# A decoder layer on one core: modulation order, 20 up-projection halves ahead, V moved ahead of sparse attention

## The chip, the cores and the metric

The kernel runs on one core of a Trainium2 chip. The time is device microseconds of one execution, from the first to the last instruction with what lies around them; a lower time is better. The core has a matrix engine (PE, with its weight loads as PEld), a vector engine (DVE), a scalar engine (ACT), a queue (SP) that issues all loads here, and 16 DMA engines.

## The reference

One decoder layer on 256 positions of width 2048, with a condition vector c that scales, shifts and gates each part (six times 2048 columns of modulation). Attention has eight stick-breaking heads and eight heads of sparse attention with an indexer; the feed-forward part has 43 pairs (gate and value) of 128 columns, a causal convolution of width 3, and a down-projection.

```python
mod = jax.nn.silu(c) @ w_ada[l] + b_ada[l]
sh1, sc1, g1, sh2, sc2, g2 = jnp.split(mod[:, None, :], 6, axis=-1)
h = rmsnorm(x, norm1_g[l]) * (1.0 + sc1) + sh1
proj = h @ w_in[l]
...
o_sb = stick_breaking_attention(q_sb, k_sb, v_sb).reshape(B, S, SB_WIDTH)
...
o_ds = dsa_attention(q_ds, k_ds, v_ds, q_ix, k_ix, w_ix * idx_scale).reshape(B, S, DSA_WIDTH)
merged = jnp.concatenate([rmsnorm(o_sb, sb_norm_g[l]), rmsnorm(o_ds, dsa_norm_g[l])], axis=-1)
x = x + g1 * (merged @ w_out[l])
h2 = rmsnorm(x, norm2_g[l]) * (1.0 + sc2) + sh2
x = x + g2 * conv_ffn(h2, w_up[l], conv_w[l], conv_b[l], w_down[l])
```

## The kernel before

Everything is held transposed, 128 features on the partitions and 256 positions along the free side. All weights are float32 and come once from HBM, in loads of 1 MB (`load`, L135) into a ring of four buffers `raw`. Each load is split (`split`, L143) into a high part, a cast on ACT (L149), and a low part, a difference on DVE (L150), for three products per tile. `nat` (L153) and `trn` (L175) issue them as three matmuls, `trn` with 256 columns each; `fold` (L161) puts two of them into one matmul with 512 columns (L172), with the low weights at 256 columns (L170), and needs two PSUM banks per pair.

The modulation has 96 tiles of 128 columns, numbered 0 to 95: sh1, sc1, g1, sh2, sc2, g2, 16 each. Most are single columns of `ada` (L227): one load `wa` and one DVE instruction with an accumulator (L229). Five groups of four columns (`PEG`, starting at 4, 40, 48, 76 and 52) are done on PE by `ada_pe` (L198): four loads `wg`, four matmuls on four column strips after each (L206), a copy on ACT (L211), four transposes (L214) and a sum on DVE. Where these pieces fall is written out by hand: `pump` (L382) is called after each load or step and takes as many single columns and group quarters as the next digit of the two strings of `PLAN` says, and by fixed rates afterwards. `need` (L395) emits a column that is due at once.

The stages follow each other: the first projection over the first eight feature tiles (A, then A2, V and QK, pass 0) and over the other eight (A and A2, pass 1; `do_A` L412, `do_V` L461, `do_QK` L467); sparse attention (rotary, index scores, top-k, softmax) with PSUM pool `psB`, four banks `acc` for projections and four `att` for attention; V and QK of pass 1 with one stick-breaking head (`sb_head`, L670) after each QK; the output projection in eight tiles O, whose first half needs only the sparse heads (`do_O`, L714; four tiles are started ahead); the residual (`resid`, L738) and its norm (`rms_b`, L109); `h2_make` (L772), which makes one of 16 tiles of h2 from two columns of modulation; the up-projection U (`do_U`, L804); and the down-projection W. For the first `G0` = 8 pairs, `do_U(f, 0)` over features 0 to 7 runs ahead, while h2 of features 8 to 15 is still being made; each of these pairs keeps one of eight PSUM banks until `do_U(f, 1)`.

Tile's scheduler sets the order of each engine's instructions when the kernel is built: of those it takes to be ready it issues the one that comes first in the program.

## Time and profile before

| | us |
|---|---|
| median of 3 runs (1203.34 to 1205.74) | 1203.6 |
| the profiled execution | 1204.37 |
| its span, first to last instruction | 1202.6 |
| PE busy | 1150.5 |
| DVE busy | 880.1 |
| ACT busy | 635.3 |
| mean granted clock of PE | 0.982 |

Busy time is the time in which an engine has at least one instruction under way. A granted clock of 1.00 is 2.4 GHz, of 0.50 is 1.2 GHz. In a timeline row the number in brackets at the end is the idle time of that engine just before, and what ended it.

### The profile page before, as it was taken

Reading aid. Unit: us, or ns where it says so; the run is one execution under the profiler, and the core shown is the slowest. Engines: PE = TensorE matmul, PEld = TensorE weight load, DVE = VectorE, ACT = ScalarE, POOL = GpSimd, SP = SyncE. Lnnn points to the kernel's source line nnn. Section 1 sums busy time; section 2 is a strip of 40 time slices with the busy share of each in tenths; the row PEclk is TensorE's granted clock in tenths of the full one; section 3 lists DMA queues with packets and bytes.
Section 4 is the critical chain, followed back from the end, with each engine's and each line's share of the span. In section 5 each row is a group of like instructions: output and inputs, shape, how many; then the busy total and the mean of one; then the engine's idle time right before and its main releaser. Section 6 shows DMA issues by size and latency. Waiting matters only on the chain.

```text
span 1202.6 us, 17743 instructions
## 1 busy us (share of the span) xinstructions
PE 1150.5 (96%) x7120; PEld 1014.9 (84%) x7120; DVE 880.1 (73%) x1267; ACT 635.3 (53%) x1004; POOL 0.2 (0%) x4
## 2 busy tenths in 40 slices
PE   4699999899999998999999999999999999999996
PEld 2578997668879997999888888888888888888885
DVE  4886788699868888978788878787787645545453
ACT  3356554458566444556665565565556544444441
POOL 0000000000000000000000000000000000000000
PEclk9799999999999998999999999999999999999998
DMA  8988989758788796966578657565665555455531
GB/s 321 365 322 318 340 331 350 288 198 328 279 314 321 295 344 250 353 227 231 187 283 313 229 207 264 211 241 213 242 214 184 201 180 202 179 193 193 181 135 70
DMA packets 43283, 303.49 MB, mean 252 GB/s; under 512 B 4928, under 2 KB 5440, under 8 KB 7232
## 3 DMA queue, kind: packets, MB, share of 16 engines
q1 hardware_dynamic: 43200, 302.35, 68.2%
q8 instruction: 56, 0.92, 0.3%
q14 instruction: 27, 0.22, 0.0%
HBM read 300.24 MB, written 2.10 MB: 251 GB/s over the span
## 4 chain that ended last, share of the span: by engine, by line
PE 91%; DVE 4%; ACT 3%; DMA 1%; issue 1%; SPq 0%; DVEq 0%
PE U L172 21%; PE W L172 13%; PE U L170 11%; PE W L170 7%; PE U L178 3%; PE U L179 3%; PE QK L177 3%; PE U L177 3%; PE O L177 3%; PE O L179 3%; PE O L178 3%; PE QK L178 3%; PE QK L179 3%; PE A L155 2%; DVE wa L229 2%; PE A L156 2%
## 5 line engine op out<-in xcount | busy, mean ns | idle before, releaser
L229 DVE SCALAR_TENSOR_TENSOR wa<-wa,scb 128x2048 f32<-128x2048 f32 x76 | 173.4, 2284 | 2.2 <-DMA wa<-wa 2.1
L848 ACT COPY u<-U 128x256 f32<-128x256 f32 x70 | 26.1, 372 | 116.6 <-PE U L172 116.6
L849 DVE TENSOR_TENSOR u<-U,u 128x256 f32<-128x256 f32 x70 | 29.4, 420 | 58.7 <-ACT u L848 58.7
L859 DVE SCALAR_TENSOR_TENSOR uc<-u,par,uc 128x255 f32<-128x255 f32 (+1 forms) x140 | 63.8, 478 | 0.9
L855 ACT ACTIVATE uc<-u,par 128x256 f32<-128x256 f32 x70 | 41.9, 601 | 0.0
L866 ACT CAST aT<-uc 128x256 fp32r<-128x256 f32 x43 | 17.4, 404 | 33.3 <-DVE uc L865 33.3
L894 DVE SCALAR_TENSOR_TENSOR x1T<-W,mod,x1T 128x256 f32<-128x256 f32 x16 | 7.7, 482 | 31.1 <-PE W L170 31.1
L745 ACT ACTIVATE x2q<-x1T 128x256 f32<-128x256 f32 x15 | 6.3, 418 | 38.7 <-DVE x1T L740 38.6
L327 ACT ACTIVATE amul<-mod,b,par 128x1 f32<-128x1 f32 x32 | 12.0, 385 | 27.7 <-DVE wa L229 27.7
L206 PE MATMUL ap<-wg,csil 128*32 128x512 f32 x160 | 24.0, 657 | 0.7 <-DMA wg<-wg 0.4
L861 ACT ACTIVATE uc<-uc 128x256 f32<-128x256 f32 x43 | 17.9, 416 | 7.7 <-DVE uc L859 7.6
L330 ACT ACTIVATE mod<-mod,par 128x1 f32<-128x1 f32 x32 | 8.7, 295 | 24.0 <-DVE wa L229 22.9
L865 DVE TENSOR_TENSOR uc<-uc 128x256 f32<-128x256 f32 x43 | 18.2, 423 | 2.8
L867 DVE TENSOR_TENSOR aT<-uc,aT 128x256 fp32r<-128x256 f32 x43 | 18.0, 418 | 0.8 <-ACT aT L866 0.7
L859 DVE SCALAR_TENSOR_TENSOR uc<-U,par,uc 128x255 f32<-128x255 f32 (+1 forms) x32 | 15.0, 478 | 1.0 <-ACT uc L855 0.6
L206 PEld LDWEIGHTS ap<-wg,csil 128*32 128x32 f32 x160 | 4.4, 116 | 9.8 <-issue 7.4
L559 PE MATMUL rel<-ws,qixT 64*128 64x128 f32 (+1 forms) x64 | 9.7, 399 | 1.5 <-ACT rl L564 1.5
L576 DVE SCALAR_TENSOR_TENSOR scw<-rl,wix,scw 128x128 f32<-128x128 f32 (+1 forms) x28 | 10.4, 409 | 0.0
L287 PE MATMUL cb<-ident,csil 128*128 128x128 f32 x16 | 3.6, 423 | 7.1 <-DMA ident<-ident 7.1
L211 ACT COPY rw<-ap 128x512 f32<-128x512 f32 x5 | 2.9, 586 | 14.1 <-PE ap L206 14.1
L155 PE MATMUL A<-wA00h,hh 128*128 128x512 f32 x4 | 2.5, 671 | 8.1 <-ACT hh L322 8.1
L855 ACT ACTIVATE uc<-U,par 128x256 f32<-128x256 f32 x16 | 9.0, 560 | 2.3 <-DVE uc L859 2.3
(2810 smaller groups left out, 4025.3 us busy)
## 6 DMA issues: line engine op xcount, KB each, us to landing
wU<-wU SPq DMA_DIRECT2D x86, 1024.0 KB, 4.8
wa<-wa SPq DMA_DIRECT2D x76, 1024.0 KB, 5.8
wD<-wD SPq DMA_DIRECT2D x43, 1024.0 KB, 4.6
wg<-wg SPq DMA_DIRECT2D x20, 1024.0 KB, 7.2
wA<-wA SPq DMA_DIRECT2D x16, 1024.0 KB, 7.4
wQK<-wQK SPq DMA_DIRECT2D x16, 1024.0 KB, 6.6
wO<-wO SPq DMA_DIRECT2D x16, 1024.0 KB, 6.9
xT<-xT SPq DMA_DIRECT2D x4, 512.0 KB, 5.8
```

What stands on the lines that cost most here:

```text
L155: T.matmul(pt, lhsT=xh, rhs=wh, start=first, stop=False)
L170: T.matmul(pt[:, 1, :], lhsT=wl, rhs=x[:, 0, :], start=False, stop=stop)
L172: T.matmul(pt, lhsT=wh, rhs=x, start=first, stop=stop)
L177: T.matmul(pt, lhsT=wh, rhs=xh, start=first, stop=False)
L178: T.matmul(pt, lhsT=wh, rhs=xl, start=False, stop=False)
L179: T.matmul(pt, lhsT=wl, rhs=xh, start=False, stop=last)
L206: T.matmul(pt[32 * j:32 * j + 32, :], lhsT=csil[:, k:k + 1].to_broadcast([P, 32]), rhs=w[:, j * 512:(j + 1) * 512], start=q == 0, stop=q == 3)
L229: i = V.scalar_tensor_tensor(out=w, in0=w, scalar=1.0, in1=scb, op0=ALU.mult, op1=ALU.mult, accum_out=mod[:, j:j + 1])
L848: A.copy(out=u[:, gv, :], in_=acc[gv][:, 1, :])
L849: V.tensor_tensor(out=u[:, gv, :], in0=acc[gv][:, 0, :], in1=u[:, gv, :], op=ALU.add)
L855: A.activation(uc[:, gv, :], u[:, gv, :], AF.Identity, scale=par[:, PCW + 3 * i + 2:PCW + 3 * i + 3], bias=par[:, PCB + i:PCB + i + 1])
L859: V.scalar_tensor_tensor(out=uc[:, gv, sft:S], in0=u[:, gv, 0:S - sft], scalar=par[:, o:o + 1], in1=uc[:, gv, sft:S], op0=ALU.mult, op1=AL ...
```

## The change

Three groups of modulation instead of five are done on PE: 4, 40 and 44. `PLAN` and the rates are gone; `pump` is now called ahead of each weight load and decides from three running estimates (`clk`) of how far PE, DVE and DMA have got, which `load`, `nat`, `trn`, `fold` and other steps advance. Groups on PE are taken only from the sparse attention on. `G0` becomes 20: each first half goes through one PSUM bank to SBUF (tiles `ut`) by a copy on ACT, and the second half is added to it on DVE. V of pass 1 stands ahead of sparse attention. PSUM pool `psB` has five banks `acc` and three `att`, and five O tiles are started ahead. The chains of sparse attention, `rms_b`, `rope`, `put`, `norm_o`, `sb_head`, `resid` and the products of `h2_make` are marked (`ahead`, `begin`, `end`), so that the scheduler takes them as if they stood at the start of the program. The code of `do_QK` is simplified without another result for parts of eight tiles.

```diff
-PEG = [4, 40, 48, 76, 52]
+PEG = [4, 40, 44]
...
+G0 = 20
...
+    def ahead(f):
+        def g(*args, **kw):
+            with tc.high_priority():
+                return f(*args, **kw)
+        return g
+    guard = []
+    def begin():
+        guard.append(tc.high_priority())
+        guard[-1].__enter__()
+    def end():
+        guard.pop().__exit__(None, None, None)
...
+    clk = {"pe": 0.0, "dve": 0.0, "dma": 8.0}
+    def spend(pe=0.0, dve=0.0):
+        clk["pe"] += pe
+        clk["dve"] = max(clk["dve"], clk["pe"] - 10.0) + dve
+    def load(src, n, name, weight=True):
+        if weight:
+            pump()
+        clk["dma"] = max(clk["dma"], clk["pe"] - 14.0) + 3.04 * n / 2048
+        if weight:
+            clk["pe"] = max(clk["pe"], clk["dma"] + 5.0)
+            spend(0.0, 2.45 * n / 2048)
...
     def pump():
+        for _ in range(2):
+            if clk["dma"] + 11.5 > clk["pe"]:
+                return
+            if pending and clk["dve"] + 6.0 <= clk["pe"]:
+                emit(pending)
             else:
+                if pend_pe and open_pe[0]:
+                    emit(pend_pe)
+                return
...
-    psum_pool[0] = (pool2, {"acc": 4, "att": 4})
+    psum_pool[0] = (pool2, {"acc": 5, "att": 3})
     ptag[0] = "acc"
+    open_pe[0] = True
+    for g in range(2):
+        do_V(last_p, g)
+    begin()
...
-    for g in range(2):
-        do_V(last_p, g)
     for h in range(NH):
         do_QK(last_p, h)
         pump()
...
-    acc = [ps(f"O{m}", tag="acc") for m in range(4)]
-    for m in range(4):
+    acc = [ps(f"O{m}", tag="acc") for m in range(5)]
+    for m in range(5):
...
-        modulate(h2[k // 4][:, k % 4, 0, :], h2[k // 4][:, k % 4, 1, :], x1T[i][:, j, :], am, r2p if k < 3 else r2, sh,
+        ahead(modulate)(h2[k // 4][:, k % 4, 0, :], h2[k // 4][:, k % 4, 1, :], x1T[i][:, j, :], am, r2p if k < 3 else r2, sh,
...
-    G0 = 8
-    uacc = {}
+    uacc, ut = {}, []
...
+        if f < G0:
+            uacc[f] = bank(f"U{f}{i}")
+        elif i == 0:
+            uacc[f] = [bank(f"U{f}{gv}") for gv in range(2)]
...
         do_U(f, 0)
-        pump()
+        if f % 4 == 0:
+            ut.append(b8([P, 4, 2, S], F32, f"ut{f}"))
+        A.copy(out=ut[-1][:, f % 4, :, :], in_=uacc.pop(f))
...
-            u = acc
+            u = ut[f // 4][:, f % 4, :, :]
+            V.tensor_tensor(out=u, in0=acc, in1=u, op=ALU.add)
```

## Rows read from the trace of the kernel before

**Rows 1.** The page, busy times and shares of the span.

```profile
PE 1150.5 (96%) x7120; PEld 1014.9 (84%) x7120; DVE 880.1 (73%) x1267; ACT 635.3 (53%) x1004; POOL 0.2 (0%) x4
```

**Rows 2.** Busy times by stage; first column is the stretch, then its length.

```profile
core 0: us, PE busy (x) PEld busy (x) DVE busy (x) ACT busy (x) POOL busy (x), PEclk, DMA share, GB/s
34.27:92.80 58.53, 50.98 (x192) 39.10 (x193) 48.19 (x56) 28.73 (x48) 0.00 (x0) 0.89 0.90 341
213.00:301.70 88.70, 83.18 (x505) 62.91 (x504) 75.57 (x184) 52.41 (x125) 0.00 (x0) 0.96 0.73 272
301.70:458.60 156.90, 156.59 (x1224) 144.26 (x1223) 125.44 (x156) 85.03 (x143) 0.00 (x0) 1.00 0.84 312
458.60:465.60 7.00, 2.12 (x16) 1.63 (x14) 4.34 (x11) 4.92 (x10) 0.00 (x0) 0.86 0.56 204
465.60:560.40 94.80, 94.44 (x769) 94.15 (x770) 83.73 (x118) 52.64 (x81) 0.00 (x0) 0.97 0.74 274
560.40:949.40 389.00, 389.00 (x2243) 344.53 (x2242) 306.29 (x453) 227.08 (x351) 0.00 (x0) 1.00 0.64 231
1188.40:1202.60 14.20, 2.53 (x16) 1.99 (x14) 6.28 (x11) 1.39 (x4) 0.00 (x0) 0.58 0.38 149
```

**Rows 3.** Groups of instructions (busy, mean ns, idle before), and one timeline row.

```profile
L229 DVE SCALAR_TENSOR_TENSOR wa<-wa,scb 128x2048 f32<-128x2048 f32 x76 | 173.4, 2284 | 2.2 <-DMA wa<-wa 2.1
L206 PE MATMUL ap<-wg,csil 128*32 128x512 f32 x160 | 24.0, 657 | 0.7 <-DMA wg<-wg 0.4
L214 PE MATMUL aq<-ident,rw 128*128 128x128 f32 x20 | 3.2, 284 | 3.6 <-ACT rw L211 3.6
L211 ACT COPY rw<-ap 128x512 f32<-128x512 f32 x5 | 2.9, 586 | 14.1 <-PE ap L206 14.1
...
358.66 1.92 PE L206 MATMUL ap<-wg,csil 128*32 128x512 f32 x14
```

**Rows 4.** Timeline of PE in the up-projection: start, length, instruction.

```profile
520.05 0.28 PE L177 MATMUL U<-h,wU110h 128*128 128x256 f32 x1
...
560.37 0.40 PE L172 MATMUL U<-h,wU800h 128*128 128x512 f32 x1
...
571.51 0.39 PE L172 MATMUL U<-h,wU900h 128*128 128x512 f32 x1
```

**Rows 5.** Timelines of SP, PE and ACT in the first projection pass.

```profile
24.87 12.13 SPq L137 DMA_DIRECT2D wa<-wa  x4
38.88 2.88 SPq L137 DMA_DIRECT2D wA<-wA  x2
48.56 0.79 PE L155 MATMUL A<-wA10h,hh 128*128 128x512 f32 x1 [5.64 <-ACT wA10h L149]
64.32 1.05 ACT L149 CAST wA40h<-wA 128x1024 fp32r<-128x1024 f32 x1
68.72 0.39 PE L155 MATMUL A<-wA40h,hh 128*128 128x512 f32 x1
```

**Rows 6.** Sparse attention: V's first split on DVE, and busy times of one stretch.

```profile
230.75 1.23 DVE L150 TENSOR_TENSOR V1000l<-V10w,V1000h 128x1024 fp32r<-128x1024 f32 x1 [3.48 <-ACT V1000h L149]
...
234.90:241.70 6.80, 6.80 (x22) 3.94 (x21) 6.80 (x24) 3.36 (x6) 0.00 (x0) 0.50 0.34 139
```

**Rows 7.** Timelines of DVE and PE ahead of the up-projection.

```profile
462.77 1.23 DVE L150 TENSOR_TENSOR wU001l<-wU,wU001h 128x1024 fp32r<-128x1024 f32 x1 [0.38 <-ACT wU001h L149]
463.91 0.48 DVE L316 SCALAR_TENSOR_TENSOR g<-x1T,amul,r2b 128x256 f32<-128x256 f32 x1
465.63 0.58 PE L177 MATMUL U<-h,wU000h 128*128 128x256 f32 x1 [2.76 <-ACT h L317]
```

**Rows 8.** Second halves of eight pairs: busy times, and groups of DVE instructions.

```profile
514.00:560.00 46.00, 46.00 (x385) 46.00 (x385) 37.06 (x57) 28.61 (x44) 0.00 (x0) 1.00 0.63 226
...
L357 DVE TENSOR_TENSOR vsb<-V,vsb 128x512 f32<-128x512 f32 x4 | 2.8, 691 | 0.0
L849 DVE TENSOR_TENSOR u<-U,u 128x256 f32<-128x256 f32 x70 | 29.4, 420 | 58.7 <-ACT u L848 58.7
```

More of the change, by code (lines that the diff above doesn't have):

```diff
@@ L107, in rb @@
         return wp.tile([P, S], F32, name=name, tag="rb", bufs=2)
+    @ahead
     def rms_b(sqs_, width, y, name, tag):
@@ L161, in fold @@
     def fold(steps):
+        spend(0.348 * len(steps))
         lo_first = narrow[0] and not any(s[4] for s in steps)
@@ L202, in ada_pe @@
         pt = st[j0]
-        w = load(a["wg"][PEG.index(j0), q], 2048, f"wg{j0}{q}")
+        w = load(a["wg"][PEG.index(j0), q], 2048, f"wg{j0}{q}", False)
+        spend(0.85 if q < 3 else 1.4)
         for j in range(4):
@@ L227, in ada @@
     def ada(j):
-        w = load(a["wa"][j], 2048, f"wa{j}")
+        w = load(a["wa"][j], 2048, f"wa{j}", False)
+        spend(0.0, 2.4)
         i = V.scalar_tensor_tensor(out=w, in0=w, scalar=1.0, in1=scb, op0=ALU.mult, op1=ALU.mult,
@@ L297, in layer @@
                            op1=ALU.mult)
+    @ahead
     def rope(x, t, H, rd, o, name):
@@ L348, in layer @@
     qk = [b8([P, 8, S], F32, f"qk{i}") for i in range(2)]
+    @ahead
     def put(half, dst, src, scale=1.0):
@@ L378, in emit @@
             emitted.update(range(j, j + 4))
-    step = [0]
+    open_pe = [False]
     def pump():
-        i = step[0]
-        step[0] += 1
-        for c, l in enumerate((pending, pend_pe)):
-            if i < len(PLAN[c]):
-                n = int(PLAN[c][i])
-            else:
-                credit[c] += RATE[c]
-                n = int(credit[c])
-                credit[c] -= n
-            for _ in range(min(n, len(l))):
-                emit(l)
+        for _ in range(2):
[3 more added lines that the diff above has]
+                emit(pending)
+            else:
+                if pend_pe and open_pe[0]:
+                    emit(pend_pe)
+                return
     def need(j):
@@ L542, in layer @@
     sc_n = [0]
+    end()
     pump()
+    begin()
     def sc_t(L, name):
@@ L587, in layer @@
         V.tensor_tensor(out=mb[t], in0=mb[t], in1=cmt, op=ALU.add)
+        end()
         pump()
+        begin()
     for t in range(NT):
@@ L646, in layer @@
                 A.activation(od[:, h, t * P:(t + 1) * P], pv[:, j, :], AF.Copy, scale=par[:, PDG + h:PDG + h + 1])
+        spend(10.0, 8.0)
+        end()
         pump()
+        begin()
     for w_ in (4, 2):
@@ L653, in layer @@
     odl = b8([P, NH, S], F32R, "odl")
+    @ahead
     def norm_o(o, rb_, oh, ol):
@@ L661, in norm_o @@
             V.tensor_tensor(out=ol[:, sl, :], in0=o[:, sl, :], in1=oh[:, sl, :].bitcast(F32), op=ALU.subtract)
+            spend(0.0, 2.5)
     norm_o(od, rdb, odh, odl)
+    end()
     pump()
+    begin()
+    end()
     os_ = b8([P, NH, S], F32, "os")
     sbt = b8([P, D], F32, "sbt")
+    @ahead
     def sb_head(h):
+        spend(3.0, 1.6)
         q = qk[h // 4][:, (h % 4) * 2, :]
@@ L736, in layer @@
     sq2 = ws[:, 1536:1792]
+    @ahead
     def resid(dst, acc, gate, res, sqsum, k, name):
+        spend(0.0, 0.9)
         resid_i[0] = V.scalar_tensor_tensor(out=dst, in0=acc, scalar=gate, in1=res, op0=ALU.mult, op1=ALU.add)
@@ L799, in layer @@
     aT = []
-    G0 = 8
-    uacc = {}
+    uacc, ut = {}, []
     def do_U(f, i):
-        if i == 0:
-            uacc[f] = [bank(f"U{f}{gv}") for gv in range(2)] if f >= G0 else bank(f"U{f}")
+        if f < G0:
+            uacc[f] = bank(f"U{f}{i}")
+        elif i == 0:
+            uacc[f] = [bank(f"U{f}{gv}") for gv in range(2)]
         w = load(a["wU"][f, i], 2048, f"wU{f}{i}")
```

39 lines of the change are left out of this document (18 added, 21 removed).

## The prediction, made before the change was run

> **What bounds the kernel now.** I read four views in this order. The page's busy line first: the matrix engine holds 1150.5 of the span's 1202.6 us, the vector engine 880.1 [rows 1]. Then the busy times by stage, to see where the missing 52 us lie: 7.5 us in the first projection pass, 5.5 us around the sparse attention, 4.9 us before the up-projection, 11.7 us in the tail, 0.7 us in all the other rows of that group, and the rest ahead of 34 us, where nothing changes [rows 2]. So from 93 us to 1188 us the end is set by the amount of matrix work and by some 11 us of waiting. Next the single waits (rows 5 to 7), then the granted clock: it stands at 0.50 for 6.8 us from 234.9 us although the engine is busy there without a gap [rows 6].
>
> The profiled execution took 1204.4 us, 1.8 us more than its span, and the median of the runs shown is 0.8 us below it. I sum against 1204.4 and take 0.8 off at the end.
>
> **The change part by part.**
>
> *Five groups of modulation on the matrix engine become three.* A group is 16 matmuls, each with two records, and four transposes. From the page a group is (24.0 + 3.2)/5 = 5.4 us busy; in place, among other matmuls, two of its four steps displace 1.92 us, so a group costs 3.8 us and its transposes 0.6 us [rows 3]. Two groups fewer: -8.4 to -10.9 us. They lie on the engine that sets the end; I take **-9.0**, near the value in place. In exchange the vector engine gets eight more columns of 2.28 us, 18.3 us in all [rows 3], in stages where it is busy 79 to 88% [rows 2]; the loads are equal, 1 MB per column either way. I cost them at nothing as long as the vector engine keeps up, which is rival 3.
>
> *Twenty pairs ahead instead of eight.* The 12 pairs that move go from the form with a 512-column matmul to three 256-column ones. A half pair of the second form takes 5.76 us (seven of them between wU110 and wU800), so a pair 11.52 us; a pair of the first form takes 571.51 - 560.37 = 11.14 us [rows 4]. 12 x 0.38 = **+4.6**. The copies of the first half to SBUF are 20 x 0.59 us on the scalar engine [rows 3], which is busy 56% there [rows 2]; that work hides them, and without it a copy would only hold a PSUM bank longer, of which eight now rotate where before all eight were held. The sums that join the halves are 20 x 0.69 us on the vector engine, in place of nothing for the first eight pairs and of two 0.42 us sums for the others [rows 8].
>
> *Modulation by running estimates instead of the written plan.* Working the new arithmetic through the loops (it gives an order of loads, no time): in the first pass the columns are emitted only by need, at most two per step, so wA of step 1 stands behind two columns instead of four; of the columns for the up-projection the 16 of its first half are out before its first load, and 15 of the other 16 come between the 20 half pairs, the last straight after them. Before, four columns were queued ahead of wA1 (the x4 row), wA1 was issued at 38.88 us, and the matrix engine waited 5.64 us for its cast [rows 5]. Later steps need the same set of loads in both orders, so most of this 5.6 us cannot be kept: step 4 had its cast done by 64.32 + 1.05 = 65.37 us and started at 68.72 us only because the engine was late [rows 5]. If the later steps follow their loads, 68.72 - 65.37 = 3.4 us remain. Ends: -5.6 (the whole wait goes) and 0 (short gaps return at steps 2 and 3, and the half clock with them); I take **-3.4**.
>
> *V ahead of sparse attention.* In before V's first low half came only at 230.75 us, after 3.5 us in which the vector engine waited for its cast [rows 6]. Now V's loads and splits stand before the rotary steps, so its 96 matmuls can fill the 5.5 us of idle time of this stage [rows 2]. Some of that is the wait of a group's transposes for a scalar copy (3.6 us in all four of them [rows 3]), and two groups still run here. I take **-2.5**, ends 0 and -5.5. The stretch at half clock costs 6.8 x 0.5 = 3.4 us of work [rows 6]; denser V work before it may avert it. I take **-2.0**, ends 0 and -3.4. The attention's own matmuls get three banks instead of four; with V and QK as filler and its result needed only at the output projection, I cost that at nothing; if the filler ran out, each wait would be like the few of this stage, inside the ends above.
>
> *Marked chains.* A mark lets a step pass earlier work that is ready too. Where chains already went first nothing moves. One place where they did not: before the up-projection, the split of wU001 runs from 462.77 us and the first product of h2 follows at 463.91 us, and the matrix engine waits 2.76 us for that h2 [rows 7]. 463.91 - 462.77 = **-1.1**; ends -2.8 and 0. What is queued behind the marked products is the split itself, and its user is the second quarter of the first half pair.
>
> *Five O banks* give one more output tile before the last attention heads are normalized. From 301.7 us to 458.6 us the matrix engine idles 0.3 us in all [rows 2], so there is nothing to win; the bank replaces the filler of the removed groups. 0.
>
> *What the trace does not show:* the second halves of 20 pairs with the joining sum. The vector engine spent 37.06 us on eight such halves, one column of 2.28 us among it [rows 8]: (37.06 - 2.28)/8 = 4.4 us, 4.7 us with the evacuation that falls outside, plus 0.69 us gives 5.0 to 5.4 us of the 5.76 us that a half takes. Lower bound 0; upper bound, if each half waits as the pairs of the other form do, 58.7/35 = 1.7 us [rows 8]: 20 x (5.3 + 1.7 - 5.76) = 24.8 us. I take **+1.5**, near the lower end, because in the stretch from 514 us the matrix engine never waited.
>
> Sum: 1204.4 - 9.0 + 4.6 - 3.4 - 2.5 - 2.0 - 1.1 + 1.5 = 1192.5; less 0.8, **1191.7 us**.
>
> The row of the stage with three matmuls per step shows weight loads busy 94.15 of 94.80 us, that of the other form 344.53 of 389.00 us [rows 2]. The Trainium skill (Perfetto Trace Analysis, Identifying the Most-Contended Engine) says that matmul busy time is a poor measure of headroom and that the busy share of the weight loads is to be used. By that rule the other form could go down to its weight loads, 344.53/35 = 9.84 us a pair, against 94.15/94.80 x 11.52 = 11.44 us, the move of 12 pairs would cost 19.2 us instead of 4.6 us, and the total would be 1206.3 us. The starts in [rows 4], 11.14 us apart in a stage without waits, speak against it: that form is paced by its columns; I give it 1 in 100, inside rival 3.
>
> **The rivals.**
>
> 1, *the forecast*: the matrix work shrinks by 4.4 us and the waits mostly close. 1185 to 1197 us, chance 0.45.
>
> 2, *only the matrix work arrives*. The marks change nothing, since chains went first already, and the gaps of the first pass come back as shorter gaps at steps 2 to 4. For it: the loads of the first pass are the same in number, and 341 GB/s flow there [rows 2]. Against it: step 4 was ready 3.4 us before it ran [rows 5]. 1204.4 - 9.0 + 4.6 - 0.8 = 1199.2 us, 1197 to 1202; chance 0.23.
>
> 3, *the vector engine becomes the bound in the second halves of the 20 pairs*, and the end is slower than before. Every half there lasts as long as the vector engine takes for two splits, the joining sum and the evacuation. Without the allowance the sum is 1190.2 us; each 0.1 us above 5.76 us costs 2 us. Up to a half of 6.4 us the result stays near 1203 us or below; from 6.6 us on (1190.2 + 20 x 0.8 = 1206.2) it is slower; at 7.0 us, 1215 us. For it: the margin falls from about 1 us to about 0.4 us a half, and the sum adds a wait of its own for the matrix engine. Against it: eight PSUM banks let the matrix engine run ahead of evacuation, and waits shrink when the vector engine is the late one. Chance 0.22, of which 0.13 slower.
>
> 4, *everything closes*: all ends below zero, 1204.4 - 10.9 + 4.6 - 5.6 - 5.5 - 3.4 - 2.8 - 0.8 = 1180.0 us; 1179 to 1185, chance 0.10.
>
> **How the numbers follow.** Runs of this kernel can tell about 0.2% from no change, that is 1201.2 to 1206.0 us. Faster: 0.45 + 0.20 of rival 2 + 0.01 of rival 3 + 0.10 = 0.76. Same: 0.03 of rival 2 and 0.08 of rival 3 = 0.11. Slower: 0.13. The range from 1182 to 1204 us leaves out the slower part of rival 3, half of rival 4 and a little beside, about 0.2.
>
> **What would show it.** Right: ap rows 96 instead of 160 and two groups less between 301 and 369 us; U's first pairs still 5.76 us a half up to pair 20, all of them without a wait; the wait of A for wA1 gone and the second projection part begun some 3 us earlier; no half clock between 220 and 250 us; the first U matmul about 1 us sooner after the last of O. Wrong: halves above 5.8 us after pair 0 comes back, with waits for splits (rival 3); new waits of A for its casts or of h for its column at steps 2 to 7 (rival 2); a wait at the first second half for the last column, which is loaded behind the last ahead half.

## The result: 1 % slower, where 1 % faster was forecast

The changed kernel takes 1217.9 us (median of 4 runs, 1216.3 to 1219.3) against 1204.5 us for the kernel before on the same chip: ratio 1.0104, 95 % interval 1.0090 to 1.0118. The forecast was 1191.7 us, with 1182 to 1204 us as its range. The profiled execution took 1216.3 us with a span of 1214.5 us, 11.9 us longer than the span of before; the forecast had been about as much shorter. So some 24 us have to be found.

The page of the changed kernel, busy line (compare [rows 1]: the matrix engine is busy for 2 us more, where the sum had its work shrink by 4.4 us):

```profile
PE 1152.5 (95%) x7432; PEld 1033.6 (85%) x7432; DVE 900.5 (74%) x1277; ACT 632.5 (52%) x998; POOL 0.2 (0%) x4
```

Busy times by stage of the changed kernel: first projection pass, rest up to the end of the second, sparse attention, QK with the attention heads, output projection, the step to the up-projection, its 20 first halves and their second halves, the other pairs.

```profile
core 0: us, PE busy (x) PEld busy (x) DVE busy (x) ACT busy (x) POOL busy (x), PEclk, DMA share, GB/s
34.27:94.64 60.37, 50.97 (x194) 39.16 (x195) 49.18 (x56) 28.53 (x48) 0.00 (x0) 0.90 0.91 335
94.64:216.30 121.66, 120.01 (x723) 107.25 (x722) 94.77 (x98) 63.02 (x100) 0.00 (x0) 1.00 0.89 332
216.30:308.00 91.70, 84.31 (x477) 59.97 (x476) 70.52 (x175) 49.86 (x120) 0.00 (x0) 0.96 0.63 241
308.00:360.86 52.86, 52.86 (x392) 49.39 (x393) 44.72 (x58) 32.94 (x62) 0.00 (x0) 1.00 0.66 230
360.86:459.40 98.54, 98.23 (x799) 96.36 (x797) 82.00 (x100) 49.18 (x78) 0.00 (x0) 1.00 0.83 304
459.40:466.57 7.17, 2.09 (x12) 1.56 (x12) 4.69 (x11) 4.95 (x10) 0.00 (x0) 0.69 0.14 31
466.57:697.00 230.43, 230.41 (x1897) 230.12 (x1898) 198.74 (x272) 134.34 (x204) 0.00 (x0) 0.99 0.72 260
697.00:961.90 264.90, 260.85 (x1498) 229.88 (x1498) 213.53 (x313) 150.17 (x234) 0.00 (x0) 1.00 0.70 246
```

The kernel before, cut at the same events (first projection pass; sparse attention, QK with the heads, output projection; the two halves of the up-projection, here cut at 696 us); [rows 2] cuts some of them a little earlier:

```profile
34.27:92.98 58.71, 51.16 (x194) 39.26 (x195) 48.37 (x56) 28.91 (x48) 0.00 (x0) 0.89 0.90 341
212.97:305.50 92.53, 87.01 (x535) 66.67 (x535) 78.95 (x187) 54.83 (x129) 0.00 (x0) 0.96 0.72 269
305.50:360.50 55.00, 54.90 (x390) 44.33 (x388) 40.04 (x57) 32.79 (x64) 0.00 (x0) 1.00 0.83 304
360.50:458.74 98.24, 98.03 (x808) 96.33 (x805) 82.05 (x96) 49.82 (x77) 0.00 (x0) 1.00 0.87 321
465.63:696.00 230.37, 230.04 (x1546) 214.11 (x1547) 196.71 (x282) 132.59 (x206) 0.00 (x0) 0.99 0.70 260
696.00:949.50 253.50, 253.50 (x1464) 224.67 (x1463) 193.38 (x289) 147.20 (x227) 0.00 (x0) 1.00 0.61 220
```

Stretch by stretch, against the terms of the sum:

| stretch (ends in the changed kernel, us) | before | after | change | forecast |
|---|---|---|---|---|
| first projection pass (94.6) | 58.7 | 60.4 | +1.7 | -3.4 |
| to the end of the second (216.3) | 120.0 | 121.7 | +1.7 | 0 |
| sparse attention, QK, output projection (459.4) | 245.8 | 243.1 | -2.7 | -13.5 |
| to the first U matmul (466.6) | 6.9 | 7.2 | +0.3 | -1.1 |
| up-projection (961.9) | 483.9 | 495.3 | +11.4 | +6.1 |
| down-projection and tail | 253.1 | 252.6 | -0.5 | 0 |

**The up-projection** lost most. The starts of pairs on the matrix engine (compare [rows 4]):

```profile
538.55 0.28 PE L207 MATMUL U<-h,wU1200h 128*128 128x256 f32 x1
...
699.83 0.40 PE L201 MATMUL U<-h,wU2000h 128*128 128x512 f32 x1
...
733.33 0.39 PE L201 MATMUL U<-h,wU2300h 128*128 128x512 f32 x1
...
756.99 0.39 PE L201 MATMUL U<-h,wU2500h 128*128 128x512 f32 x1
```

From half 12 to pair 20 stand 28 halves: (699.83 - 538.55)/28 = 5.76 us, first and second halves alike. So the second halves, where rival 3 looked for trouble, show no delay. The trouble comes after them: pairs 23 and 24 together took 23.66 us instead of 2 x 11.11. It sits in every second pair: 24, 26, 28, 30, 32 and 34 lost 0.5 to 1.6 us each, and over pairs 22 to 35 the loss is 6.2 us. Where this comes from, in four views of one place: the DMA queue's issues, the vector engine, the scalar engine, the matrix engine.

```profile
739.69 0.33 SPq L164 DMA_DIRECT2D wa<-wa  x1
```

```profile
743.24 0.42 DVE L905 TENSOR_TENSOR u<-U,u 128x256 f32<-128x256 f32 x1 [0.27 <-ACT u L904]
746.13 2.29 DVE L261 SCALAR_TENSOR_TENSOR wa<-wa,scb 128x2048 f32<-128x2048 f32 x1 [2.47 <-DMA wa<-wa]
...
751.00 1.22 DVE L177 TENSOR_TENSOR wU2411l<-wU,wU2411h 128x1024 fp32r<-128x1024 f32 x1
```

```profile
744.91 1.05 ACT L176 CAST wU2411h<-wU 128x1024 fp32r<-128x1024 f32 x1
```

```profile
752.28 1.22 PE L199 MATMUL U<-h,wU2411l 128*128 128x256 f32 x8 [0.71 <-DVE wU2411l L177]
```

A column's load was issued at 739.69 us and landed at about 746.1 us. Its product already stood at the head of the vector engine's queue, which idled 2.47 us there. The splits of wU24 stood behind it: the cast that the last of them needs was done at 745.96 us, but this split began at 751.00 us, and the matrix engine waited for it. The row of these products over the whole execution has 32.1 us of idle time where [rows 3] shows 2.2 us:

```profile
L261 DVE SCALAR_TENSOR_TENSOR wa<-wa,scb 128x2048 f32<-128x2048 f32 x84 | 192.1, 2287 | 32.1 <-DMA wa<-wa 31.8
```

The new estimates emit one column for each pair from 21 to 35, fifteen in a row; 19.8 us of the idle time stand there.

**The first pass.** The wait of step 1 fell from 5.64 us [rows 5] to 1.41 us, as forecast, but steps 2 and 3 wait now (matrix engine, then vector engine):

```profile
43.66 1.20 PE L183 MATMUL A<-wA10h,hh 128*128 128x512 f32 x4 [1.41 <-ACT hh L356]
53.04 1.22 PE L183 MATMUL A<-wA20h,hh 128*128 128x512 f32 x2 [3.59 <-ACT hh L356]
62.42 0.50 PE L183 MATMUL A<-wA30h,hh 128*128 128x512 f32 x1 [2.19 <-ACT hh L356]
```

```profile
55.33 2.28 DVE L261 SCALAR_TENSOR_TENSOR wa<-wa,scb 128x2048 f32<-128x2048 f32 x1
...
57.88 2.28 DVE L261 SCALAR_TENSOR_TENSOR wa<-wa,scb 128x2048 f32<-128x2048 f32 x1
...
62.10 1.23 DVE L177 TENSOR_TENSOR wA30l<-wA,wA30h 128x1024 fp32r<-128x1024 f32 x1 [1.93 <-ACT wA30h L176]
```

Two columns, the modulation on the scalar engine, the cast and the split stand one after another in each step, 9.4 us a step (62.42 - 53.04), because a step's columns are now made only in that step. There is a rival: three loads of 1 MB, as many as a step has, take 9.4 us too at the 335 GB/s of this pass. The run a_look below decides between them.

**Sparse attention.** Half clock has not gone, it has moved (0.50 for 6.8 us before [rows 6], twice 3.4 us now), each time behind a wait of the matrix engine; the second is a wait for wQK10, whose load stands behind five loads of groups:

```profile
226.70:230.10 3.40, 3.30 (x8) 2.63 (x9) 3.33 (x9) 1.04 (x1) 0.00 (x0) 0.50 0.99 417
277.90:281.30 3.40, 3.20 (x7) 1.19 (x7) 1.41 (x3) 2.71 (x13) 0.00 (x0) 0.50 0.98 414
```

```profile
278.10 0.58 PE L207 MATMUL QK<-hh,wQK100h 128*128 128x256 f32 x1 [3.19 <-ACT wQK100h L176]
```

**Before the up-projection** the marks changed nothing: the split of wU001 still stands ahead of the first product of h2, and the wait is the 2.76 us of [rows 7]:

```profile
463.39 1.23 DVE L177 TENSOR_TENSOR wU001l<-wU,wU001h 128x1024 fp32r<-128x1024 f32 x1 [0.38 <-ACT wU001h L176]
464.53 1.26 DVE L350 SCALAR_TENSOR_TENSOR g<-x1T,amul,r2b 128x256 f32<-128x256 f32 x3
```

```profile
466.57 0.58 PE L207 MATMUL U<-h,wU000h 128*128 128x256 f32 x1 [2.76 <-ACT h L351]
```

### The profile page after: what moved, and what is told of

Read it like the earlier page. It is cut to its first block, busy times and chain, and to the rows that moved or that the text cites. A ratio compares the mean times of both kernels' runs of the same rounds, so it can differ in the third digit from the quotient of the medians.

```text
span 1214.5 us, 18418 instructions
## 1 busy us (share of the span) xinstructions
PE 1152.5 (95%) x7432; PEld 1033.6 (85%) x7432; DVE 900.5 (74%) x1277; ACT 632.5 (52%) x998; POOL 0.2 (0%) x4
## 4 chain that ended last, share of the span: by engine, by line
PE 69%; DVE 15%; DMA 7%; ACT 4%; issue 4%; SPq 0%; DVEq 0%; ACTq 0%
PE W L201 13%; PE W L199 7%; DMA wa<-wa 6%; PE U L207 6%; PE U L208 6%; DVE wa L261 6%; PE U L209 6%; PE U L201 6%; PE U L199 3%; PE O L208 2%; PE O L209 2%; PE O L207 2%; PE QK L209 2%; PE QK L207 2%; PE QK L208 2%
## 5 line engine op out<-in xcount | busy, mean ns | idle before, releaser
L261 DVE SCALAR_TENSOR_TENSOR wa<-wa,scb 128x2048 f32<-128x2048 f32 x84 | 192.1, 2287 | 32.1 <-DMA wa<-wa 31.8
L904 ACT COPY u<-U 128x256 f32<-128x256 f32 x46 | 17.1, 372 | 50.6 <-PE U L201 50.6
L916 DVE SCALAR_TENSOR_TENSOR uc<-u,par,uc 128x255 f32<-128x255 f32 x92 | 42.0, 478 | 0.3
L912 ACT ACTIVATE uc<-u,par 128x256 f32<-128x256 f32 x46 | 27.7, 601 | 21.4 <-DVE u L905 21.4
L905 DVE TENSOR_TENSOR u<-U,u 128x256 f32<-128x256 f32 x46 | 19.4, 422 | 24.8 <-ACT u L904 24.7
L916 DVE SCALAR_TENSOR_TENSOR uc<-ut,par,uc 128x255 f32<-128x255 f32 (+1 forms) x80 | 33.2, 478 | 0.0
L912 ACT ACTIVATE uc<-ut,par 128x256 f32<-128x256 f32 x40 | 21.8, 593 | 0.1
L908 DVE TENSOR_TENSOR ut<-U,ut 128x512 f32<-128x512 f32 x20 | 13.8, 691 | 6.4 <-PE U L209 6.4
L237 PE MATMUL ap<-wg,csil 128*32 128x512 f32 x96 | 16.4, 669 | 0.0
L890 ACT COPY ut<-U 128x512 f32<-128x512 f32 x20 | 11.6, 578 | 0.0
```

Source lines behind the costliest of these rows:

```text
L261: i = V.scalar_tensor_tensor(out=w, in0=w, scalar=1.0, in1=scb, op0=ALU.mult, op1=ALU.mult, accum_out=mod[:, j:j + 1])
L905: V.tensor_tensor(out=u[:, gv, :], in0=acc[gv][:, 0, :], in1=u[:, gv, :], op=ALU.add)
L912: A.activation(uc[:, gv, :], u[:, gv, :], AF.Identity, scale=par[:, PCW + 3 * i + 2:PCW + 3 * i + 3], bias=par[:, PCB + i:PCB + i + 1])
L916: V.scalar_tensor_tensor(out=uc[:, gv, sft:S], in0=u[:, gv, 0:S - sft], scalar=par[:, o:o + 1], in1=uc[:, gv, sft:S], op0=ALU.mult, op1=AL ...
```

## The experiments

Labels with b_ are the kernel before plus parts of the change, those with a_ the changed kernel with something undone or mended. Stage lengths below are from one profiled execution each (us), ratios are to the kernel before on the same chip with their 95 % interval. "Middle" is the stretch from the end of the second projection pass to the end of the output projection.

How far a single execution can be trusted is read from four kernels: after, a_thin, a_defer and a_noload differ only in the second loop of the up-projection, and up to the end of the output projection their engines run the same instructions in the same order. Their middles took 243.1, 242.0, 245.7 and 243.3 us. So a difference of less than some 4 us in the column "middle" says nothing by itself.

| kernel | what | ratio | first pass | middle | up-projection |
|---|---|---|---|---|---|
| before | | 1 | 58.7 | 245.8 | 483.9 |
| after | all parts | 1.0104 (1.009 to 1.0118) | 60.4 | 243.1 | 495.3 |
| b_g20 | 20 pairs ahead | 1.0036 (1.0023 to 1.005) | 59.2 | 246.2 | 488.4 |
| b_peg3 | three groups | 1.004 (1.0027 to 1.0052) | 58.9 | 243.4 | 489.7 |
| b_peg3b5 | and five O banks | 1.004 (1.0025 to 1.0055) | 59.1 | 242.1 | 492.3 |
| b_vahead | V ahead | 1.0202 (1.0188 to 1.0216) | 58.8 | 270.0 | 483.8 |
| b_marks | marks | 1.0117 (1.0098 to 1.0135) | 58.6 | 258.9 | 483.6 |
| b_marks2 | marks, columns later | 1.0174 (1.0152 to 1.0196) | 58.2 | 262.5 | 483.6 |
| b_mv | marks and V ahead | 1.0351 (1.0335 to 1.0367) | 58.2 | 289.3 | 483.8 |
| b_all4 | all but the estimates | 1.0434 (1.0409 to 1.0458) | 59.2 | 289.8 | 492.1 |
| a_thin | last columns spread | 1.0038 (1.0025 to 1.0052) | 60.4 | 242.0 | 489.1 |
| a_defer | products later in program | 1.0096 (1.008 to 1.0112) | 60.4 | 245.7 | 494.2 |
| a_noload | products without loads | 1.0045 (1.0029 to 1.0062) | 60.4 | 243.3 | 488.8 |
| a_look | four columns ahead in pass 1 | 1.0091 (1.0075 to 1.0106) | 58.3 | 245.8 | 497.6 |
| a_open | groups held back | 1.0102 (1.0085 to 1.0118) | 60.4 | 243.3 | 494.6 |
| a_vlate | V back | 1.0097 (1.0079 to 1.0115) | 60.4 | 243.0 | 494.9 |
| a_nomarks | no marks | 1.0221 (1.0199 to 1.0243) | 60.4 | 260.2 | 495.2 |
| a_plain | no marks, V back, two mends | 1.0182 (1.0155 to 1.0208) | 58.6 | 262.8 | 488.2 |
| a_peg5 | five groups | 1.0168 (1.0152 to 1.0184) | 60.3 | 258.1 | 488.4 |
| a_tl16 | two mends, 16 pairs ahead | 1.0054 (1.004 to 1.0067) | 58.9 | 243.0 | 491.6 |

### One part at a time on the kernel before

**b_g20**: `G0 = 20`, first halves through `ut`, the last sixteen columns spread over the later pairs (five products fall into the second halves of the 20 pairs).

> The kernel before with one part of the change alone: the first halves of 20 pairs ahead through SBUF instead of 8 in PSUM; groups, written plan, marks, V and banks stay as before, and the last sixteen columns are spread evenly over pairs 5 to 42. Theory one: the only cost is the form, 12 pairs x 0.38 us, so the up-projection grows by 4 to 6 us over the 483.9 us of before and the whole by 4 to 6 us (ratio 1.003 to 1.005), with halves of 5.76 us. Theory two: the vector engine is late in the second halves; they last 6.2 us or more and the whole grows by over 10 us. Theory three (the weight loads pace the other form): over 15 us.

The up-projection grew by 4.5 us, and every half of the 20 pairs, first or second, starts 5.76 us after the last. Theory one: the form is the only cost. The joining sums and the copies are hidden, as costed.

**b_peg3** (and eight more columns in `PLAN`):

```
-PEG = [4, 40, 48, 76, 52]
+PEG = [4, 40, 44]
```

> The kernel before with three modulation groups on the matrix engine (columns 4, 40, 44) instead of five, under the written plan, with eight more columns written into the plan in the output projection and the first halves of the up-projection. Theory one: the term of the prediction holds by itself and two groups fewer give 7 to 9 us (ratio 0.992 to 0.994). Theory two: the eight columns on the vector engine come back as waits for splits, so that 3 us or less remain (ratio 0.9975 to 1.003). The trace tells: ap records 96, and the waits of the output projection and of the first 8 half pairs above 0.3 us in theory two only.

Theory two, and more: 5 us slower. The matrix engine reaches the output projection 16.9 us sooner (343.7 instead of 360.5 us) and then waits for the attention heads, at half clock for part of it:

```profile
377.10 0.58 PE L115 MATMUL rsbp<-nones,ws 128*128 128x1 f32 x4 [1.04 <-DVE ws L700]
379.37 0.40 PE L129 MATMUL rsbb<-ident,rsby 128*128 128x128 f32 x2 [1.69 <-DVE rsby L126]
383.70 0.58 PE L177 MATMUL O<-osh,wO010h 128*128 128x256 f32 x1 [3.93 <-ACT osh L660]
```

```profile
343.70:390.00 46.30, 39.17 (x271) 36.49 (x271) 37.47 (x45) 24.82 (x47) 0.00 (x0) 0.90 0.76 288
```

In before the first use of osh was at 389.5 us, and the first of its two casts, which is all that the first use waits for (in b_peg3 it comes 0.05 us after that cast), stood ready not long before:

```profile
380.06 1.05 ACT L660 CAST osh<-os 128x1024 fp32r<-128x1024 f32 x1 [0.20 <-DVE os L658]
```

So the matrix engine there had 389.5 - 381.1 = 8.4 us in hand against the chain of sparse attention, eight heads and norm, and the roughly 9 us of two groups are more than that. The stage of before without any idle time had a second path 8 us below the first. In b_peg3 the chain itself also came 2.5 us later (this cast was done at 383.65 us; the heads took 75 instead of 67 us). The middle is 2.4 us shorter than in before, no more than single executions differ. The rest of the loss is in the up-projection, +5.8 us: ten columns instead of seven now stand beside the first eight halves, and the last of these and the first second half take 8.1 instead of 5.76 us.

**b_peg3b5**: the same with `{"acc": 5, "att": 3}` and five first O tiles.

> The kernel with three groups alone, and in addition five O banks and three for the attention. Theory one, that the groups were the filler under the last attention heads and a fifth output tile takes their place: the waits of rsbp, rsbb and osh in the output projection (1.0, 1.7 and 3.9 us with three groups alone) and the half clock behind them go, 5 to 8 us faster than with three groups alone (1202.5 to 1205.5 us, ratio to before 0.998 to 1.0005). Theory two: with three banks the heads themselves come later and the waits stay; within 2 us of 1210.4.

The time did not change (1210.4 both times): waits of 3.1 and 2.8 us take the place of the three above. The bank is worth nothing that these runs can tell, as the prediction had it.

**b_vahead**: `do_V(last_p, g)` ahead of the first `rope`, plan places moved along.

> The kernel before with V's second half ahead of the sparse attention, its four places in the written plan moved with it; all else as before. Theory one: the idle time and the half clock of the sparse attention only change their owner, and the whole stays within 1.5 us (ratio 0.9988 to 1.0012). Theory two, the prediction's: 2.5 us of idle time and 2 us of half clock go, 4 to 5 us faster (ratio about 0.996).

Neither: 24 us slower. V's splits pass the sparse chain, whose first transpose comes at 253.2 instead of 226.8 us; the matrix engine idles 6.4 us for a later one of its transposes, and then has waits of 3.4 and 2.8 us before the second O tiles, because the heads end at 401.5 instead of 368.6 us:

```profile
279.68 0.45 PE L596 MATMUL kdsp<-ident,ws 128*128 128x128 f32 x1 [6.37 <-DVE ws L310]
```

**b_marks**: `@ahead` and `begin()`/`end()` as in the change.

> The kernel before with the marks alone (the chains of the sparse attention, norms, evacuations, attention heads, residuals and modulation put first). Theory one: the chains went first already or end on the same waits, so it stays within 1.5 us (ratio 0.9988 to 1.0012); the gap from the last output-projection matmul to the first of the up-projection stays 6.9 to 7.2 us. Theory two, the prediction's: that gap shrinks by 1.1 us. Theory three: the marked products and chains hold up splits queued behind them and the sparse attention gets 2 us or more slower.

Theory three by its sign, 13 us slower, though not by splits. On the vector engine the marked chain's short steps alternate with columns of 2.28 us:

```profile
288.61 0.69 DVE L645 TENSOR_REDUCE nm<-lg 128x2 f32<-128x512 f32 x1 [0.17 <-PE lg L642]
289.22 2.28 DVE L246 SCALAR_TENSOR_TENSOR wa<-wa,scb 128x2048 f32<-128x2048 f32 x1
...
291.43 0.16 DVE L651 RECIPROCAL rec<-sum 128x2 f32<-128x2 f32 x1
291.51 0.67 DVE L645 TENSOR_REDUCE nm<-lg 128x2 f32<-128x512 f32 x1
292.09 2.28 DVE L246 SCALAR_TENSOR_TENSOR wa<-wa,scb 128x2048 f32<-128x2048 f32 x1
```

Each reciprocal waits for a column that got between. The logits take 28 us instead of 17, and the heads begin at 318 instead of 302 us. A mark puts a step first only among what is ready; here something long got in between two steps of a chain.

**b_marks2**: in the plan of columns `0222000110020002` becomes `0000001111222110` (second QK pass).

> The kernel before with the marks, and with the twelve columns that the written plan puts into the second QK pass moved from heads 0 to 7 to heads 3 to 7, so that fewer are ready beside the sparse chain. Theory one (columns between the chain's short steps stretch it: 261.6 to 278.6 us became 263.3 to 291.4 us): the chain's logits take 20 us or less, the norm of the sparse heads comes before 310 us instead of 318, and at most 5 us of the 13 remain (ratio to before 0.998 to 1.004). Theory two (the marks themselves misorder the chain): 1214 us or more.

The chain answered as theory one has it in part: the logits take 23.6 us, the norm comes at 309 us. But the whole became slower still: ten columns instead of seven stand beside the heads now, which take 73.5 instead of 69.6 us, and the output projection begins 13 us later. So columns between the chain's steps stretch it, but how much of the 13 us is due to them stays open: taken away from there, they cost more beside the heads.

**b_mv**: both, on the kernel before.

> The kernel before with both the marks and V ahead of the sparse attention, under the written plan with V's places moved along, five groups, four O banks. Theory one (they need each other: V's splits pass the sparse chains unless these are marked, and the marked chains need V as work beside them): within 5 us of before (ratio 0.997 to 1.004). Theory two (the costs add): 30 us or more slower. Theory three (the written plan puts columns and groups ahead of the marked chains whatever V does): 10 to 20 us slower, as with the marks alone.

Theory two: 24 + 13 = 37 us were to be expected if the costs add, 42 us came. Marks do not help V ahead under the written plan: seven columns stand in the stretch before the logits, which begin at 302 instead of 262 us.

**b_all4**: all parts but the estimates, `G0 = 16`.

> The written plan instead of the estimates under all other parts of the change: three groups, V ahead, marks, five O banks, and 16 pairs ahead through SBUF (one column for each of the first 15 halves, none but two in the second halves, 0.6 for each later pair). Theory one (each part only pays beside the others, and the estimates are what loses in the changed kernel): up to the end of the output projection 4 to 9 us sooner than before (450 to 455 us), the up-projection 3 us longer than before, the whole 1198 to 1203 us, faster than both. Theory two (the written plan's places do not fit the new order either): the output projection ends at 458 us or later and the whole is 1206 us or more.

My theory one fell at once: 52 us slower, with the middle as long as in b_mv. The written plan's columns meet the new order: eight of them stand before the logits, five beside them. Under the estimates, in the changed kernel, the vector engine has none between 260 and 308 us.

### Undoing and mending parts of the changed kernel

**a_thin**, in `pump()` for the second loop:

```
+            if pending and (n in (6, 14) or n >= 20 and (n - 20) % 3 == 0):
+                emit(pending)
```

> The changed kernel with the last columns spread over the second loop of the up-projection by count (at its 7th and 15th load, then one for every third load from pair 20 on) instead of by the estimates (one for every pair from 21 to 35). Theory one, that the pairs that hold a column overrun because the vector engine stands at a column whose load has not landed: pairs 23 to 35 come back to 5.54 to 5.6 us a half, 4 to 6 us of the 6.2 go (1212 to 1214 us, ratio to the kernel before about 1.006). Theory two, that the overrun has another cause (such as the joining of the two accumulators): no change, 1217 to 1219 us.

Theory one: every start of pairs 20 to 42 is 5.54 to 5.58 us after the last, and the up-projection falls by the whole 6.2 us, to 489.1 us. The whole falls to 1210.1 us, 2 us below the range given; where these 2 us come from, no run shows. The idle time in front of the products:

```profile
L261 DVE SCALAR_TENSOR_TENSOR wa<-wa,scb 128x2048 f32<-128x2048 f32 x84 | 192.0, 2286 | 9.3 <-DMA wa<-wa 8.9
```

**a_defer**: the product is emitted after the next wU instead of at once.

> The changed kernel with each column of the second loop loaded where it is, but its product put one load of wU later in the program, so that the number of columns per pair and all transfers stay and only the place in the vector engine's queue moves. Theory one (the head of the queue waits for the transfer): the 20 us of idle time ahead of these products fall below 5 us and 3 to 6 us of the 6.2 us go. Theory two (too much vector work in a pair): idle time goes, but the pairs still take over 11.4 us; within 1.5 us of 1217.9. Theory three: the longer-held load buffer delays the next wU and it gets slower by 2 us or more.

No verdict: the order written out for the vector engine hardly moved (the product still stands between the two sums of a pair, at 771.07 us after 1.95 us of idle time), so the cause it was to move stayed where it was.

**a_noload**: in the second loop `out=scb, in0=scb, scalar=0.0, in1=scb` instead of a loaded column.

> The changed kernel, where the fifteen columns of the second loop of the up-projection are products of a tile that is resident (the last gate's values are therefore not computed): the same vector work in the same places of the program, no load and no wait for one. Theory one (head of the queue waits for the transfer): all pairs run at 5.54 to 5.6 us a half and 5 to 7 us go, 1211 to 1213 us. Theory two (one column per pair is too much vector work): pairs 23 to 35 still take 11.3 us or more, and less than 2 us go.

Pairs 20 to 42 run at 5.54 to 5.58 us a half, and 7.5 us go, 6.5 of them in the up-projection. As nothing had to be waited for, the sixteen products stand earlier, from 577 to 748 us, so it is not the same place, and sixteen loads are gone with the waits; but the rival of too much vector work is answered the better so. Busy times of a part of the second halves and of the next two pairs:

```profile
582.00:697.00 115.00, 115.00 (x961) 115.00 (x960) 114.75 (x184) 75.75 (x117) 0.00 (x0) 1.00 0.51 180
697.00:720.00 23.00, 23.00 (x144) 20.79 (x143) 23.00 (x35) 12.82 (x20) 0.00 (x0) 1.00 0.55 202
```

The vector engine is busy 114.75 of 115 us and the matrix engine never waits. Vector work that is ready fills every gap here without cost; a product that waits for its load at the head of the queue is what costs.

**a_look**, behind step 0 of the first pass:

```
+            if pi == 0 and j == 0:
+                for _ in range(4):
+                    emit(pending)
```

> The changed kernel with four columns queued behind step 0 of the first projection pass, as the written plan of before had it. Theory one (one step of look-ahead is what the estimates lack): the waits of A for the modulated input at steps 2 to 7 (9.4 us in all) shrink, step 1 waits longer again, and A's first pass ends 1.5 to 3 us sooner; the whole gains as much, 1215 to 1216.5 us. Theory two (the loads themselves bound the pass): within 0.5 us of 94.6 us at its end.

Theory one for the pass: 58.3 us, 0.4 less than before, with step 1 waiting 6.16 us again. With the same loads, in another order, the pass is 2.1 us shorter than in the changed kernel and the DMA engines move 344 instead of 335 GB/s, so 335 GB/s was not the limit of the loads. The whole took 1215.7 us, 2.2 us less, but its interval (1.0075 to 1.0106) overlaps that of the changed kernel: whether the whole gained is not shown.

**a_open**: `open_pe[0] = True` moved behind the sparse attention.

> The changed kernel with the two groups of the matrix engine held back until the sparse attention's own code is past, so that the loads of wQK10 and its like stand ahead of them. Theory one: the wait of 3.2 us for wQK10 and the half clock behind it go, and the groups cost 4.4 instead of 5.7 us each: 3 to 6 us faster, 1212 to 1215 us. Theory two: the groups were the filler of the sparse attention, its chains leave the matrix engine idle in their place, and the whole stays within 1.5 us or gets slower.

Theory two: the wait for wQK10 is gone, and the middle is 243.3 us, 243.1 in the changed kernel. The groups fill the sparse attention in one order, QK in the other.

**a_peg5**: `PEG = [4, 40, 48, 76, 52]` in the changed kernel.

> The changed kernel with the five groups of before on the matrix engine. Ten of the fifteen columns of the second loop of the up-projection are then done earlier, so its 6.2 us of overrun shrink to about 2 us in any theory; the front is read from the end of the output projection (459.4 us in the changed kernel). Theory one (the term of the prediction is real beside the other parts): it ends 7 to 10 us later. Theory two (the groups were filler): 0 to 3 us later, and the whole is faster than the changed kernel by 2 to 4 us.

Theory one, by more than its number: the output projection ends 15.0 us later. Two groups save 15 us here and 2.4 us in the kernel before: with five groups the first cast of osh is done at 398.2 us and first used at 410.6 us, 12.5 us in hand; without two of them 6.6 us are left (388.5 to 395.0 us), so no wait takes their place.

**a_vlate**: V back behind the sparse attention, the marks kept.

> The changed kernel with V's second half back behind the sparse attention, marks and estimates kept. Theory one (V is the work beside the marked chains): the sparse attention's idle time grows from 7.4 us to 15 us or more, and the whole is 5 us or more slower than the changed kernel. Theory two (V ahead only delays the chains, whose first transposes came at 236.4 instead of 226.8 us): the last attention heads end some 6 us sooner and the whole is 0 to 4 us faster.

Theory two's end of its range: 1216.8 us, 1 us faster, which its interval does not tell from no change. The chains do come 6 us sooner (heads from 302 us), but the heads then take 73.4 instead of 67.4 us. V ahead is worth nothing that can be told here, once the chains are marked.

**a_nomarks**:

```
-            with tc.high_priority():
-                return f(*args, **kw)
+            return f(*args, **kw)
```

> The changed kernel without its marks. Theory one (V ahead of the sparse attention alone cost 24 us because its splits pass the sparse chains; the marks undo that): 10 to 25 us slower than the changed kernel, the sparse chains and the heads late, and the output projection waits for them. Theory two (the marks do nothing or hurt, as they do alone on the kernel before): within 2 us, or faster.

Theory one by its time: 15 us slower, and the middle is 17 us longer. The same marks that cost 13 us in the middle of the kernel before save 17 us here.

**a_plain**: neither marks nor V ahead, with the mends of a_thin and a_look.

> The changed kernel without the marks and with V behind the sparse attention as before, and with the two mended losses (columns of the second loop spread out, four columns queued behind step 0 of the first pass). Theory one (marks and V ahead bring nothing once no column stands beside the sparse chain): 1206 to 1210 us, what the two mends alone would give. Theory two (they pay there): 1213 us or more, with waits of the output projection for the last heads. Theory three (they cost there too): 1203 us or less.

Theory two: the middle takes 262.8 us. The useful neighbour is b_peg3b5, which has the same groups, banks, order of V and no marks, under the written plan: 242.1 us. So the estimates in place of this plan lengthen the middle by 20.7 us. The first 42 us of each, a_plain first:

```profile
214.86:257.00 42.14, 28.86 (x173) 20.14 (x171) 34.81 (x121) 15.53 (x28) 0.00 (x0) 0.83 0.51 200
```

```profile
214.63:257.00 42.37, 38.53 (x239) 25.76 (x238) 32.99 (x116) 17.49 (x30) 0.00 (x0) 1.00 0.66 242
```

Under the estimates five of the eight loads of both groups go out ahead of V's first; V, which was the work beside the sparse chain, begins at 266 us only, the matrix engine idles 13.3 of 42 us, and its mean granted clock there is 0.83. The later part is in the order on the matrix engine: with no mark, the first matmul of the norm behind the last head (rsbp) stands behind all five O tiles, 11.5 us after its input ws is ready; in the changed kernel it follows at once. The vector engine and the matrix engine, in a_plain and then in the changed kernel:

```profile
390.66 0.42 DVE L759 TENSOR_TENSOR ws<-ws,sbt 128x256 f32<-128x256 f32 x1
402.62 0.28 PE L127 MATMUL rsbp<-nones,ws 128*128 128x1 f32 x2
...
376.65 0.42 DVE L753 TENSOR_TENSOR ws<-ws,sbt 128x256 f32<-128x256 f32 x1 [0.45 <-ACT sbt L752]
377.13 0.38 PE L129 MATMUL rsbp<-nones,ws 128*128 128x1 f32 x2
```

The marks repair what the estimates broke: with marks and V behind (a_vlate) the middle takes 243.0 us, with V ahead and no marks (a_nomarks) 260.2 us. In a_vlate five of the groups' loads still go ahead of V and the matrix engine still idles 9.1 of the first 42 us, so groups ahead of V are not by themselves what costs the 20.7 us.

**a_tl16**: a_thin, a_look and 16 pairs ahead, one column for each of their first halves.

> The changed kernel with the columns of the second loop spread out, four columns queued behind step 0 of the first pass, and 16 instead of 20 pairs ahead with one column for each of their halves. By the single runs: 1217.9 - 7.8 - 2.2 - 4 x 0.38 = 1206.4 us, within 0.3% of the kernel before (1203 to 1208 us). If the columns at one per half make the first halves longer than 5.76 us, 1208 to 1212 us.

The second case: 1211.8 us. With a column in nearly every half, the starts of first halves 8 to 14 lie 5.86 to 6.41 us apart, 2.8 us in all, and the first three halves take 1.4 us longer than in the changed kernel. No version found beats the kernel before.

## Why the prediction was wrong

The sign was wrong, and the range of 1182 to 1204 us did not hold the result. Of the 24 us between forecast and result 10.8 stand in the middle, 5.3 in the up-projection, 5.1 in the first pass, and the rest in two short stretches. The step that failed most is the one that took the groups' work and the idle time around V off the middle, as if nothing else could set its end. Point by point:

- **The form of 12 pairs, +4.6 us: right.** b_g20 measured +4.5 us in the up-projection, and the halves take 5.76 us. The rule of the Trainium skill that was weighed there (Perfetto Trace Analysis, Identifying the Most-Contended Engine: headroom by the busy share of the weight loads) would by the prediction's estimate have made it 19.2 us; this run does not agree with that. The allowance of +1.5 us for the vector engine was not needed.
- **Eight more columns "at nothing as long as the vector engine keeps up": the step that failed in the up-projection, +6.2 us.** The vector engine kept up where rival 3 tested it. The prediction followed the new arithmetic as far as the last column of the first halves, and did not follow it to the second loop, where it emits fifteen columns pair after pair. Nor did it ask when each load lands against the place of its product in an order fixed beforehand. a_thin and a_noload show both: spread out, or with nothing to wait for, the 6.2 us go.
- **The first pass, -3.4 us: wrong by 5.1 us.** The ends given were -5.6 and 0, with the remark that gaps could return at steps 2 and 3; they did, and 0 was no bound. The failed step is that later steps would follow their loads: they follow columns that are now made one step at a time. a_look brings the pass back to 58.3 us, so look-ahead was the thing that the written plan had and the estimates lack.
- **Two groups, -9.0 us, V ahead, -2.5 and -2.0 us: -13.5 forecast in the middle, -2.7 measured, which is no more than single executions differ by. This step failed most.** The two terms for V were read from idle time and half clock of before; both came back at other places (7.4 us of idle time in the sparse attention where there were 5.5, half clock twice for 3.4 us), and V ahead is worth nothing beside the marks (a_vlate) and costs 24 us without them under the written plan (b_vahead). The term of the groups took their matmul time for time of the whole. What two groups are worth depends on what else sets the end: 2.4 us in before (b_peg3), where the chain of the heads is close behind, 15 us in the changed kernel (a_peg5). What the rest of the change costs depends on the groups in the same way: nothing that can be told with three groups (242.1 us in b_peg3b5, 243.1 in after), 12.3 us with five (245.8 in before, 258.1 in a_peg5). The estimates by themselves cost 20.7 us (a_plain against b_peg3b5), and the marks win that back. In the prediction's sum the low end of the groups' range, 8.4 us, does not follow from its rows, which give 2 x (3.8 + 0.6) = 8.8 us; nothing hangs on it.
- **The rows of before could have warned of a part of it.** "The matrix engine idles 0.3 us in all" from 301.7 to 458.6 us [rows 2] was read as if whatever is taken from its work came off the time. The first cast of osh ended 8.4 us before its use. b_peg3 shows what that means: two groups fewer brought 6.7 us of new waits, and 2.4 us were gained.
- **Marks, -1.1 us ahead of the up-projection: wrong, +0.3 us.** The products of h2 follow the split as before: the split starts at 463.39 us, and r2b, which the products need, is done at 463.82 us only, so a mark has nothing to put first. That chains "already went first" was assumed for the other places; a_nomarks and b_marks, 17 us saved and 13 us lost, show that marks moved more than any term of the sum, in either direction.
- **Five banks, 0: right** (b_peg3b5).
- **Rival 2** (only the matrix work arrives, 1199.2 us) had the mechanism of the first pass right, and **rival 3** the culprit, the vector engine's queue, at the wrong place and as an amount of work rather than as a wait for a load.
- The loss of 1.7 us from 94.6 to 216.3 us had no term. The matrix engine shows three waits of 0.5 to 0.6 us there, one for a cast and two for splits. No run isolates it; in the runs with the estimates it lies between 0.8 and 2.1 us.

What stays open: how the 17 to 21 us that the estimates' order costs without the marks divide. Two places are seen, the groups' loads ahead of V and the norm behind the O tiles, and no run has either of them alone. The heads of 75 instead of 67 us in a_plain were not taken apart.

## What to carry to other kernels

A change that reorders work is not a sum of its parts: parts that cost 4, 5, 13 and 24 us alone, under the written plan, gave 13 us together with the estimates, where the marks repaired what the estimates broke; so price a part beside the order that it will run in. Before taking work off the busiest engine, measure how far behind it the next chain ends, which is the time from the moment its result is ready to the moment it is used. And for each load that an in-order engine consumes, compare its landing with the place of its consumer in the queue: a consumer a little too early holds up all that stands behind it.

## What was not expected of the hardware

The vector engine was busy for 114.75 of 115 us in a_noload while the matrix engine took its 5.76 us a half without a wait: a share near 100 % was no sign of a bound, while at 213.5 of 264.9 us, 81 %, in the changed kernel waits at the head of its queue held the matrix engine up. The granted clock fell to 0.50, the lower of its two levels, in the changed kernel for 3.4 us from 226.7 us and for 3.4 us from 277.9 us; ahead of the first the matrix engine had idled 1.34 us and then 0.99 us, ahead of the second 3.19 us.
